# Attention in pairs of heads, convolution low parts on GpSimd, and an eighteenth FFN pair in a hybrid decoder layer

## The chip, the cores and the metric

One core of one Trainium2 chip. The metric is the device time of one execution in microseconds (us); the kernel before was run three times.

## The reference

One layer on 512 tokens of width 1024, all in float32:

```python
h = h + 0.5 * rmsnorm(swiglu(rmsnorm(h, g1), ffn1_w_in, ffn1_w_out), g1p)   # FFN1, hidden width 2816
mix = token_mixer(rmsnorm(h, gm), ...)                                      # below
h = h + rmsnorm(mix, gmp)
h = h + 0.5 * rmsnorm(swiglu(rmsnorm(h, g2), ffn2_w_in, ffn2_w_out), g2p)   # FFN2
gate = sigmoid(rmsnorm(h, gp) @ ple_w_gate)
h = h + rmsnorm(gate * (p @ ple_w_proj), gpp)

# token_mixer: one projection of u gives q_a k_a v_a z_a a_a b_a q_b k_b v_b q_i k_i w_i g_a g_b
qkv = silu(causal_conv(concat(q_a, k_a, v_a), conv_w))      # 4 taps, 1536 channels
o_a = gated_delta_rule(l2norm(q), l2norm(k), v, g, beta)    # 8 heads, chunks of 64, a triangular solve
score = sum_h w_i * relu(q_i . k_i)                         # indexer; the top 128 admissible keys per query
o_b = softmax(q_b . k_b over the selected keys) @ v_b       # 8 heads of 64, causal
mix = (sigmoid(g_a) * (o_a' @ w_br_a) + sigmoid(g_b) * (o_b @ w_br_b)) @ w_out
```

## The kernel before, in words

**Matmuls.** A float32 product is made as three: each operand is split into a high part and a low part (the remainder), and mm3 (L99 to L102) multiplies high by high, low by high and high by low. Weights come in chunks of 128x1024: wchunk (L84 to L93) loads raw, ScalarE casts it to the high part whi (L91), VectorE subtracts for the low part wlo (L92). There are two raw buffers and three of whi and wlo, so that the cast for one chunk waits until the chunk three before it has been multiplied. Transposes run on TensorE through tr (L108).

**FFN** (ffn, Seven). f counts 22 slices of 128 hidden columns, each with gate and up. An ordinary f is two tiles pgu of 24 matmuls of 512 columns (L418 and after). From f = 5 on, Seven.pair makes gate and up together with seven half-width products instead of eight, 84 matmuls of 256 columns (pfa, pfb, pfc, pfd). It needs the tiles t, sums of blocks of the input made once after f = 3. The output projection, out_proj, ends with put(0) and put(1), transposes of the next stage's first token tiles (ys), set between the last matmuls of the last token tile: put(0) behind the six matmuls with a = 0, put(1) behind the six with a = 2.

**The mixer.** The convolution's 12 chunks run one after the other (conv_mm: 24 matmuls into pc; conv_tr: transposes pct). Each pc takes a PSUM bank that is free again when VectorE has added the last tap (cy, L521) of the chunk two before. Beside them VectorE selects the top keys (MAX8 and MATCH_REPLACE). When the keys are normed (rk, on GpSimd), the decay and beta rows go through a transpose (prow), a copy (rowT) and a DMA to DRAM (rowd, L859), from which chunk_blocks loads them broadcast: DT (L813: a load, a select on GpSimd, a subtraction on VectorE, an exponential on ScalarE) and kbr (L809: two loads, a product on VectorE). The products pA (L824, L826) of four heads per block, two of which lie in rows 0 to 63 and two in rows 64 to 127 of the array, become BT and KQs. Diagonal blocks of BT go through DRAM (dgd) to solve(), 62 dependent VectorE steps (L924, L926), whose result goes through DRAM (zd) and back for the first pw matmuls of the delta rule.

**Attention** has 32 units: four pairs of heads, each with four token tiles (tt = 3, 0, 2, 1) and two heads. att_soft makes the score pat (L881, 128 to 512 columns), adds the bias on VectorE, and exponentiates on ScalarE into at; att_tr transposes at into ppt (one to four 128x128) and copies it to pt; att_pv multiplies with the values into pob (L911). Step i issues att_soft(i), att_tr(i - 2) and att_pv(i - 3). The tile tag at has three buffers that DT and rl share; pt has two. Behind attention come ptm (the last in-projection chunks) and pw.

A scheduler at build time orders every engine's queue; program order holds only where the code asks for it.

Of the kernel before, what the change touches and what calls it, by code (L numbers as in the profile page):

```python
# [32 lines left out]
def layer_kernel(ctx, tc, x, pT, wf1, wo1, wfm, wsm, wtm, wbr, wout, wf2, wo2, wgate, wproj,  # L33
# [17 lines left out]
    env = Env()  # L51

# [30 lines left out]
    def wchunk(src, n=1024, dst=None, eng=None):  # L83
        raw = wp.tile([128, 1024], F32, name="raw", tag="raw", bufs=2)  # L84
        SY.dma_start(raw[:, :n], src)
        if dst is None:
            hi = wp.tile([128, 1024], F32R, name="whi", tag="whi", bufs=3)
            lo = wp.tile([128, 1024], F32R, name="wlo", tag="wlo", bufs=3)
        else:
            hi, lo = dst  # L90
        A.copy(hi[:, :n], raw[:, :n])  # L91
        (eng or V).tensor_sub(lo[:, :n], raw[:, :n], hi[:, :n].bitcast(F32))  # L92
        return hi, lo  # L93
# [94 lines left out]
    def out_proj(nj, load, lhs, order1, order2, held, half, ys, gp, finish, free, evac=None, lead=0, held0=0, split=False):  # L188
# [28 lines left out]
        for ch, order in ((0, order1), (1, order2)):  # L217
# [14 lines left out]
            for tt in range(4):  # L232
                cut = ((0, 256), (256, 512)) if split and ch and tt == 3 else ((0, 512),)
                for i, (lo, hi) in enumerate(cut):
                    if i:
                        ps[tt] = axp("acc2")
                    for a, j in enumerate(order[n:]):
                        if ch and tt == 3:
                            with in_order() if env.puts else ExitStack():
                                m = part(ps[tt], tt, ws[a], j, n + a == 0, n + a == nj - 1, lo, hi)  # L240
                            if a in (0, 2):
                                put(a // 2, m)
# [142 lines left out]
    def ffn(fp, free, wf, wo, hsrc, u, gi, gn_i, first, hold=None):  # L385
# [31 lines left out]
        for f in range(nf, FT):  # L417
# [3 lines left out]
            if f >= 5:  # L421
                seven.pair(f, wf[2 * f], wf[2 * f + 1], hid)
                continue
# [288 lines left out]
    for tt in (3, 2, 1):  # L712
        S = 128 * (tt + 1)
        sc = tp.tile([128, S], F32, name=f"sc{tt}")
        for hd in range(8):
# [3 lines left out]
            rl = tp.tile([128, T], F32, name="rl", tag="at", bufs=3)  # L719
# [82 lines left out]
    def chunk_blocks():  # L802

        for c in range(4):
# [6 lines left out]
            for h4 in range(2):  # L811
                DT = tp.tile([128, 4, 128], F32, name="DT", tag="at", bufs=3)
# [28 lines left out]
    late = []  # L841
    for j in list(range(4, 8)) + list(range(4)) + list(range(8, 12)):
# [25 lines left out]
    drip(99)  # L868
    for j in (13, 14, 15):
        gate_tile(j)  # L870
        next(blocks)
# [4 lines left out]
    def att_soft(i):  # L876
# [6 lines left out]
        at = tp.tile([128, T], F32, name="at", bufs=3)  # L883
# [9 lines left out]
    def att_tr(i):  # L893
# [6 lines left out]
        pt = tp.tile([128, T], F32, name="pt", bufs=2)  # L900
# [37 lines left out]
    for i in range(len(units) + 3):  # L938
        if i < len(units):
            att_soft(i)  # L940
        if i in (2, 4, 6):
            next(blocks, None)
        if i == 7:
            for _ in blocks:
                pass
            ZC, XC, Z = solve()
        if i == 1:
            conv_tr(*late.pop())
        if 0 <= i - 2 < len(units):
            att_tr(i - 2)  # L950
        if 0 <= i - 3 < len(units):
            att_pv(i - 3)
# [175 lines left out]
    if True:  # L1128
# [33 lines left out]
        def load(ch, j, a):  # L1162
            w = wchunk(wout[ch, j], dst=xo.get(a) or (upper(tl) if ch or j > 1 else None))
            if (ch, j) == (1, 3):
# [5 lines left out]
                 sandwich_tail(h, ys, gnt, u2), lambda: (tail_pool.close(), mx_pool.close()), held0=2)  # L1170
# [129 lines left out]
```

## Time and profile before

| what | value |
|---|---|
| median of three runs | 1283.7 us (1282.6 to 1284.87) |
| the profiled execution | 1280.92 us, span 1279.1 us |
| TensorE (PE) | 1253.4 us busy, 98% |
| VectorE (DVE) | 883.5 us, 69% |
| ScalarE (ACT) | 567.0 us, 44% |
| GpSimd (POOL) | 66.2 us, 5% |
| granted TensorE clock, mean | 0.996 |

Times in rows are microseconds from the start of the span. A row of a timeline gives the start, the duration, the engine, the line, the operation, what it writes and reads, and in brackets how long the engine was idle before it and what ended that. Matmuls are pipelined and a record's end is modelled, so the time that a matmul takes is read from the start of one to the start of the next. A matmul of plain float32 (a score, a pA product) is two records.

### The profile page before, as it was taken

What the parts mean: (1) busy time and instruction counts of PE and PEld (TensorE: products, weight loads), DVE (VectorE), ACT (ScalarE), POOL (GpSimd) and SP (SyncE); (2) the same over time, 40 slices, a digit from 0 to 9 for tenths busy, and PEclk for the clock granted to TensorE, in tenths of its full rate; (3) what the DMA queues carried; (4) which work ended last, traced back from release to release, by engine and by line L of the source; (5) the groups of instructions that cost most, each with busy time, mean ns of one, the idle gap of its engine ahead of it and who ended that gap; (6) DMA issues with size and microseconds to landing.
All of it is one profiled execution on the core that took longest, in us unless ns stands there. A gap on an engine that the chain in (4) does not pass through costs nothing.

```text
span 1279.1 us, 19714 instructions
## 1 busy us (share of the span) xinstructions
PE 1253.4 (98%) x7885; PEld 1103.6 (86%) x7885; DVE 883.5 (69%) x1451; ACT 567.0 (44%) x914; POOL 66.2 (5%) x69
## 2 busy tenths in 40 slices
PE   6999999999999999989999999999999999999997
PEld 6999999988889888877678888779899999888886
DVE  6779999743372799976685544758699998623555
ACT  6334444752352443454554222344344445822353
POOL 0000000000010000031002001310000000000000
PEclk9999999999999999999999999999999999999999
DMA  6323333522442223244305544732433333433331
GB/s 214 126 66 112 109 111 100 181 82 94 147 156 84 66 68 116 91 116 124 92 1 133 164 158 157 230 116 83 134 108 106 99 106 123 144 93 113 115 116 66
DMA packets 59517, 147.76 MB, mean 116 GB/s; under 512 B 17761, under 2 KB 20257, under 8 KB 59425
## 3 DMA queue, kind: packets, MB, share of 16 engines
q1 hardware_dynamic: 58992, 144.93, 35.4%
q10 hardware_dynamic: 432, 1.57, 0.4%
q8 instruction: 62, 1.02, 0.3%
q14 instruction: 31, 0.25, 0.1%
HBM read 132.81 MB, written 13.66 MB: 115 GB/s over the span
## 4 chain that ended last, share of the span: by engine, by line
PE 89%; DMA 4%; DVE 4%; ACT 2%; issue 1%; POOL 0%; SPq 0%; DVEq 0%; POOLq 0%; ACTq 0%
PE acc L101 6%; PE acc L102 6%; PE acc L100 6%; PE p L101 3%; PE p L102 3%; PE p L100 3%; PE pfd L100 3%; PE pfb L100 3%; PE pfd L102 3%; PE pfd L101 3%; PE pfb L102 3%; PE pfb L101 3%; PE pfc L100 3%; PE pfc L101 3%; PE pfc L102 2%; PE ptm L100 2%
## 5 line engine op out<-in xcount | busy, mean ns | idle before, releaser
L92 DVE TENSOR_TENSOR wlo<-raw,whi 128x1024 fp32r<-128x1024 f32 x70 | 86.9, 1241 | 62.5 <-ACT whi L91 60.0
L91 ACT CAST whi<-raw 128x1024 fp32r<-128x1024 f32 x70 | 73.5, 1051 | 122.5 <-PE pc L101 35.3
L92 DVE TENSOR_TENSOR vlo<-raw,vhi 128x1024 fp32r<-128x1024 f32 x37 | 46.8, 1267 | 78.0 <-ACT vhi L91 78.0
L102 PE MATMUL acc<-vhi,hid 128*128 128x512 f32 x240 | 93.4, 389 | 0.0
L101 PE MATMUL acc<-vlo,hid 128*128 128x512 f32 x240 | 93.4, 389 | 0.0
L100 PE MATMUL acc<-vhi,hid 128*128 128x512 f32 x240 | 81.7, 389 | 0.0
L91 ACT CAST vhi<-raw 128x1024 fp32r<-128x1024 f32 x37 | 38.7, 1048 | 83.2 <-PE acc L102 72.5
L285 ACT CAST whi<-sb 128x1024 fp32r<-128x1024 f32 x26 | 27.3, 1049 | 83.9 <-PE pfc L101 75.1
L78 POOL TENSOR_TENSOR rinv<-ms,mhalf 128x1 f32<-128x1 f32 x32 | 19.4, 606 | 801.7 <-DVE ms L123 801.7
L100 PEld LDWEIGHTS acc<-vhi,hid 128*128 128x128 f32 x240 | 45.1, 188 | 9.4
L102 PEld LDWEIGHTS acc<-vhi,hid 128*128 128x128 f32 x240 | 45.1, 188 | 9.4
L101 PEld LDWEIGHTS acc<-vlo,hid 128*128 128x128 f32 x240 | 45.0, 188 | 9.4
L101 PE MATMUL ptm<-wlo,uhi 128*128 128x512 f32 x128 | 50.3, 393 | 0.0
L100 PE MATMUL ptm<-whi,uhi 128*128 128x512 f32 x128 | 50.0, 395 | 0.0
L102 PE MATMUL ptm<-whi,ulo 128*128 128x512 f32 x128 | 49.8, 391 | 0.0
L100 PE MATMUL pc<-uhi,whi 128*128 128x512 f32 x96 | 38.5, 401 | 3.9 <-ACT DT L818 3.9
L100 PE MATMUL pg<-uhi,whi 128*128 128x512 f32 x104 | 41.2, 396 | 0.0
L102 PE MATMUL pg<-uhi,wlo 128*128 128x512 f32 x104 | 40.9, 393 | 0.0
L101 PE MATMUL pg<-ulo,whi 128*128 128x512 f32 x104 | 40.7, 392 | 0.0
L286 DVE TENSOR_TENSOR hid<-gt,hid 128x512 fp32r<-128x512 f32 x44 | 29.5, 689 | 15.1 <-ACT hid L285 15.1
L102 PE MATMUL pc<-uhi,wlo 128*128 128x512 f32 x96 | 38.9, 405 | 0.0
L101 PE MATMUL pfd<-t,x 128*128 128x256 f32 x136 | 38.4, 282 | 0.0
(536 smaller groups left out, 4210.2 us busy)
## 6 DMA issues: line engine op xcount, KB each, us to landing
raw<-wf SPq DMA_DIRECT2D x52, 512.0 KB, 3.7
raw<-wo SPq DMA_DIRECT2D x44, 512.0 KB, 3.6
rawy<-wf SPq DMA_DIRECT2D x36, 512.0 KB, 3.8
raw<-wfm SPq DMA_DIRECT2D x28, 512.0 KB, 3.8
raw<-wtm SPq DMA_DIRECT2D x20, 512.0 KB, 3.7
gd<-gst SPq DMA_DIRECT2D x16, 256.0 KB, 2.1
raw<-wbr SPq DMA_DIRECT2D x8, 512.0 KB, 4.0
grl<-gd SPq DMA_DIRECT2D x16, 256.0 KB, 3.8
```

The lines of the kernel that those rows point to most:

```text
L78: G.tensor_tensor(out_, in_, e, op=ALU.pow)
L91: A.copy(hi[:, :n], raw[:, :n])
L92: (eng or V).tensor_sub(lo[:, :n], raw[:, :n], hi[:, :n].bitcast(F32))
L100: PE.matmul(ps, l[0], r[0], start=start, stop=False)
L101: PE.matmul(ps, l[0], r[1], start=False, stop=False)
L102: return PE.matmul(ps, l[1], r[0], start=False, stop=stop)
L285: A.copy(dst[0], src)
L286: V.tensor_sub(dst[1], src, dst[0].bitcast(F32))
```

## The change

Five edits:

- the subtraction for wlo of the 12 convolution chunks goes from VectorE to GpSimd (env.split);
- pairs start at f = 4 instead of f = 5 in both FFNs;
- put(1) of the two FFNs goes behind a = 3 instead of a = 2; the mixer's own call keeps a = 2;
- the tag at gets four buffers instead of three, pt four instead of two;
- attention issues two scores, then the transposes of the two units before, then the value products of the two before those.

```diff
     env = Env()
+    env.split = V
...
-        (eng or V).tensor_sub(lo[:, :n], raw[:, :n], hi[:, :n].bitcast(F32))
+        (eng or env.split).tensor_sub(lo[:, :n], raw[:, :n], hi[:, :n].bitcast(F32))
...
-                            if a in (0, 2):
-                                put(a // 2, m)
+                            if a in (0, at):
+                                put(min(a, 1), m)
...
-            if f >= 5:
+            if f >= 4:
                 seven.pair(f, wf[2 * f], wf[2 * f + 1], hid)
...
-                DT = tp.tile([128, 4, 128], F32, name="DT", tag="at", bufs=3)
+                DT = tp.tile([128, 4, 128], F32, name="DT", tag="at", bufs=4)
...
+    env.split = G
     for j in list(range(4, 8)) + list(range(4)) + list(range(8, 12)):
...
     drip(99)
+    env.split = V
...
-        pt = tp.tile([128, T], F32, name="pt", bufs=2)
+        pt = tp.tile([128, T], F32, name="pt", bufs=4)
...
-    for i in range(len(units) + 3):
-        if i < len(units):
-            att_soft(i)
-        if i in (2, 4, 6):
-            next(blocks, None)
-        if i == 7:
-            for _ in blocks:
-                pass
-            ZC, XC, Z = solve()
-        if i == 1:
-            conv_tr(*late.pop())
-        if 0 <= i - 2 < len(units):
-            att_tr(i - 2)
-        if 0 <= i - 3 < len(units):
-            att_pv(i - 3)
+    for p in range(len(units) // 2 + 2):
+        for i in (2 * p, 2 * p + 1):
+            if i < len(units):
+                att_soft(i)
+            if i in (2, 4, 6):
+                next(blocks, None)
+            if i == 7:
+                for _ in blocks:
+                    pass
+                ZC, XC, Z = solve()
+            if i == 1:
+                conv_tr(*late.pop())
+        for back, step in ((1, att_tr), (2, att_pv)):
+            for i in (2 * (p - back), 2 * (p - back) + 1):
+                if 0 <= i < len(units):
+                    step(i)
```

GpSimd's queue from the index scores to the DT selects, before (rk is the key norm, rq the query norm):

```order
L726 AFFINE_SELECT sc_4295<-sc_4295 128x128
L78 TENSOR_TENSOR rk<-ssk,mhalf 128x32
L814 AFFINE_SELECT DT<-DT 128x512 x3
L78 TENSOR_TENSOR rq<-ssq,mhalf 128x32
L814 AFFINE_SELECT DT<-DT 128x512
```

and now:

```order
L727 AFFINE_SELECT sc_4351<-sc_4351 128x128
L93 TENSOR_TENSOR wlo<-raw,whi 128x1024 x9
L79 TENSOR_TENSOR rk<-ssk,mhalf 128x32
L93 TENSOR_TENSOR wlo<-raw,whi 128x1024 x3
L815 AFFINE_SELECT DT<-DT 128x512 x4
L79 TENSOR_TENSOR rq<-ssq,mhalf 128x32
L815 AFFINE_SELECT DT<-DT 128x512
```

Nine low parts stand ahead of rk, three more ahead of the selects, and a fourth select ahead of rq.

VectorE's queue at the first DT, about 566 to 575 us, before (the three cy are the taps of the tenth convolution chunk):

```order
L521 SCALAR_TENSOR_TENSOR cy<-pc,prm,cy 128x511
L816 TENSOR_TENSOR DT<-DT,gcs 128x512
L810 TENSOR_TENSOR kbr<-kT,kbr 128x512
L863 TENSOR_SCALAR ssq<-ssq 128x32
L521 SCALAR_TENSOR_TENSOR cy<-pc,prm,cy 128x510
L548 TENSOR_TENSOR vbt<-pct,rkb 128x4x128
L816 TENSOR_TENSOR DT<-DT,gcs 128x512 x2
L521 SCALAR_TENSOR_TENSOR cy<-pc,prm,cy 128x509
L810 TENSOR_TENSOR kbr<-kT,kbr 128x512
```

and now:

```order
L817 TENSOR_TENSOR DT<-DT,gcs 128x512
L547 TENSOR_REDUCE ssq<-sq 128x4x2
L817 TENSOR_TENSOR DT<-DT,gcs 128x512 x2
L865 TENSOR_SCALAR ssq<-ssq 128x32
L817 TENSOR_TENSOR DT<-DT,gcs 128x512
L93 TENSOR_TENSOR wlo<-raw,whi 128x1024
L811 TENSOR_TENSOR kbr<-kT,kbr 128x512
L522 SCALAR_TENSOR_TENSOR cy<-pc,prm,cy 128x511
L811 TENSOR_TENSOR kbr<-kT,kbr 128x512
L549 TENSOR_TENSOR vbt<-pct,rkb 128x4x128
L522 SCALAR_TENSOR_TENSOR cy<-pc,prm,cy 128x510
L522 SCALAR_TENSOR_TENSOR cy<-pc,prm,cy 128x509
```

Four DT subtractions now stand ahead of the first kbr product, and all three taps behind it.

TensorE's queue in attention, some 625 us into the span, before (numbers behind a name tell its buffers apart):

```order
L881 MATMUL pat_6164<-hz_4110 128x512
L108 MATMUL ppt_6173<-cst_78,at_6048 128x128 x2
L881 MATMUL pat_6182<-hz_4110 128x128
L911 MATMUL pob_6141<-vb_4771,pt_6139 128x64 x3
L911 MATMUL pob_6178<-vb_4771,pt_6158 128x64 x2
L108 MATMUL ppt_6191<-cst_78,at_6148 128x128 x4
L881 MATMUL pat_6201<-hz_4110 128x128
L108 MATMUL ppt_6210<-cst_78,at_6166 128x128 x4
```

and now:

```order
L884 MATMUL pat_6234<-hz_4166 128x128
L884 MATMUL pat_6243<-hz_4166 128x128
L914 MATMUL pob_6225<-vb_4827,pt_6190 128x64 x3
L109 MATMUL ppt_6252<-cst_78,at_6199 128x128 x4
L914 MATMUL pob_6266<-vb_4827,pt_6218 128x64 x2
L109 MATMUL ppt_6259<-cst_78,at_6208 128x128 x4
L884 MATMUL pat_6273<-hz_4166 128x384
L884 MATMUL pat_6282<-hz_4166 128x384
```

The two scores of a pair of heads stand side by side.

## Rows read from the trace of the kernel before

**Rows 1.** The page: busy time, share and instructions of each engine.

```profile
PE 1253.4 (98%) x7885; PEld 1103.6 (86%) x7885; DVE 883.5 (69%) x1451; ACT 567.0 (44%) x914; POOL 66.2 (5%) x69
```

**Rows 2.** Timeline of TensorE in FFN1: f = 4, first two pairs, put(1).

```profile
64.14 0.39 PE L100 MATMUL pgu<-uhi,whi 128*128 128x512 f32 x1
...
75.02 0.28 PE L100 MATMUL pfa<-uhi,whi 128*128 128x256 f32 x1
...
85.01 0.28 PE L100 MATMUL pfa<-uhi,whi 128*128 128x256 f32 x1
...
363.12 1.09 PE L108 MATMUL put<-cst,ys 128*128 128x128 f32 x8 [0.85 <-DVE ys L156]
```

**Rows 3.** Timeline of VectorE in FFN1: the last of the tiles t.

```profile
47.84 1.21 DVE L286 TENSOR_TENSOR t<-trys,t 128x1024 fp32r<-128x1024 f32 x1
```

**Rows 4.** Timeline of TensorE at the twelfth convolution chunk.

```profile
570.14 0.50 PE L824 MATMUL pA<-kbr,kT 64*128 64x128 f32 x4 [0.45 <-DVE kbr L810]
...
575.31 0.77 PE L100 MATMUL pc<-uhi,whi 128*128 128x512 f32 x1 [3.91 <-ACT DT L818]
...
579.71 0.39 PE L101 MATMUL pc<-ulo,whi 128*128 128x512 f32 x1
```

**Rows 5.** Timeline of VectorE: convolutions, and one row from 692.

```profile
546.27 1.23 DVE L92 TENSOR_TENSOR wlo<-raw,whi 128x1024 fp32r<-128x1024 f32 x1
...
569.40 0.68 DVE L810 TENSOR_TENSOR kbr<-kT,kbr 128x512 f32<-128x512 f32 x1
...
574.43 0.73 DVE L521 SCALAR_TENSOR_TENSOR cy<-pc,prm,cy 128x509 f32<-128x509 f32 x1
...
692.17 2.20 DVE L92 TENSOR_TENSOR wlo<-raw,whi 128x1024 fp32r<-128x1024 f32 x1 [1.25 <-ACT whi L91]
```

**Rows 6.** Timeline of GpSimd: rk, the third DT select, two-input operations.

```profile
544.97 5.43 POOL L78 TENSOR_TENSOR rk<-ssk,mhalf 128x32 f32<-128x32 f32 x1 [77.99 <-DVE ssk L848]
...
572.70 1.04 POOL L814 TENSOR_SCALAR_AFFINE_SELECT DT<-DT 128x512 f32<-128x512 f32 x1 [0.18 <-DMA DT<-rowd]
...
809.94 2.15 POOL L1151 TENSOR_TENSOR grl<-grl,ybm 128x512 f32<-128x512 f32 x1 [3.91 <-DVE grl L1150]
818.25 2.55 POOL L1151 TENSOR_TENSOR grl<-grl,ybm 128x512 f32<-128x512 f32 x2 [6.16 <-DVE grl L1150]
```

**Rows 7.** Stretches: busy us of PE, PEld, DVE, ACT, POOL; clock, DMA.

```profile
572.00:580.00 8.00, 4.69 (x12) 3.73 (x13) 6.71 (x13) 3.17 (x4) 6.96 (x3) 0.57 0.40 109
637.00:667.00 30.00, 29.95 (x180) 20.73 (x180) 24.32 (x94) 20.02 (x68) 0.00 (x0) 1.00 0.00 1
```

**Rows 8.** DMA: issue of rowd on SyncE; of tile DT, issue to landing.

```profile
561.54 0.53 SPq L859 DMA_DIRECT2D rowd<-rowT  x1
...
DMA to landing us min/median/max: 3.0/3.5/5.6
```

**Rows 9.** Groups by line on TensorE, 607 to 667: busy us, mean ns.

```profile
L881 PE MATMUL pat<-hz 64*128 64x128 f32 (+3 forms) x62 | 24.5, 475 | 0.0
```

**Rows 10.** Timeline of TensorE: pA of two heads at once, of one.

```profile
591.82 0.49 PE L824 MATMUL pA<-kbr,kT 64*128 64x128 f32 x4
592.04 0.49 PE L826 MATMUL pA<-qT,kT 64*128 64x128 f32 x4
...
609.18 0.38 PE L824 MATMUL pA<-kbr,kT 64*128 64x128 f32 x2
609.41 0.38 PE L826 MATMUL pA<-qT,kT 64*128 64x128 f32 x2
```

**Rows 11.** Timeline of VectorE: first and last step of the solve, its transposition.

```profile
635.61 0.19 DVE L924 TENSOR_TENSOR ztmp<-dz 128x31 f32<-128x31 f32 x1 [0.81 <-DMA dz<-dgd]
...
674.53 0.22 DVE L926 TENSOR_TENSOR dz<-dz,ztmp 128x31 f32<-128x31 f32 x1
...
683.39 1.25 DVE L935 STREAM_TRANSPOSE dz<-dz 128x1024 f32<-128x1024 f32 x1 [1.12 <-DMA dz<-zd]
```

**Rows 12.** Timeline of TensorE: the first matmuls of pw.

```profile
690.50 1.68 PE L996 MATMUL pw<-dz,BT 32*32 32x32 f32 x94
```

More of the change, by code (lines that the diff above doesn't have):

```diff
@@ L186, in put, with out_proj @@
                 env.puts.pop(tt)()
-    def out_proj(nj, load, lhs, order1, order2, held, half, ys, gp, finish, free, evac=None, lead=0, held0=0, split=False):
+    def out_proj(nj, load, lhs, order1, order2, held, half, ys, gp, finish, free, evac=None, lead=0, held0=0, split=False, at=3):
         sums = [sp.tile([128, 3], F32, name=f"sums{tt}", bufs=1) for tt in range(4)]
@@ L718, in layer_kernel @@
                 PE.matmul(pd[:, :S], qiT[hd][:, tt * 128:(tt + 1) * 128], kiT[i][:, :S], start=i == 0, stop=i == 1)
-            rl = tp.tile([128, T], F32, name="rl", tag="at", bufs=3)
+            rl = tp.tile([128, T], F32, name="rl", tag="at", bufs=4)
             A.activation(rl[:, :S], pd[:, :S], AF.Relu)
@@ L882, in att_soft @@
                   start=True, stop=True)
-        at = tp.tile([128, T], F32, name="at", bufs=3)
+        at = tp.tile([128, T], F32, name="at", bufs=4)
         nm = sp.tile([128, 1], F32, name="nm", bufs=4)
@@ L1169, in layer_kernel @@
                  lambda k, tk: (mgh[:, k, tk], mgl[:, k, tk]), list(range(4)), list(range(4)), 4, False, ys, gpt,
-                 sandwich_tail(h, ys, gnt, u2), lambda: (tail_pool.close(), mx_pool.close()), held0=2)
+                 sandwich_tail(h, ys, gnt, u2), lambda: (tail_pool.close(), mx_pool.close()), held0=2, at=2)
         u = u2
```

## The prediction

> **What bounds the kernel now.** I read the page first: TensorE is busy for 1253.4 of 1279.1 us [rows 1], so time is won by giving it less to do, by closing one of its few gaps, or by letting two of its matmuls run at once. Then I read the timeline of TensorE for gaps at the places that the diff touches. One stands where FFN1 ends: the transposes of ys wait 0.85 us [rows 2]. The large one is at 571: the four pA products wait 0.45 us, and the first matmul of the twelfth convolution chunk 3.91 us [rows 4]. The row gives an exponential of DT as its releaser, but that line's work had long ended; what ended at 575.2 is the last convolution tap on VectorE (cy, 509 columns, 574.43 + 0.73) [rows 5], which frees the PSUM bank that this chunk (two after the tap's own) writes. VectorE does its work in order, and ahead of that tap stand three DT subtractions, each behind a GpSimd select, each behind a DMA: the third select begins at 572.70, released by a DMA [rows 6]. After the gap the clock is low: 0.57 is the mean grant of the stretch 572 to 580 [rows 7], and ten matmuls take from 575.31 to 579.71 [rows 4], 0.44 us apiece against the 0.227 that 48 ordinary ones show (64.14 to 75.02, [rows 2]): 2.1 us more. The gap thus costs 0.45 + 3.91 + 2.1 = 6.4 us.
>
> **Attention** (607 to 667) shows no gap, so there I asked what TensorE does and who is next. VectorE is busy for 24.3 of the 30 us from 637 on [rows 7], and carries the triangular solve from 635.61 to 674.53 [rows 11] between the softmax steps. On the solve wait a few DMAs, and on those the first pw matmul at 690.50 [rows 12]; between attention and pw lie 128-column weight chunks (ptm) that need neither.
>
> **The change, part by part.** The sum is made against the profiled execution, 1280.9 us (span 1279.1 and 1.8 around it). The median shown, 1283.7, stands 2.8 above; I add that at the end.
>
> 1. One more FFN pair. An ordinary f is 48 matmuls, 64.14 to 75.02 = 10.88 us; a pair is 84 of half the width, 75.02 to 85.01 = 9.99 us [rows 2]. Twice (two FFNs) 0.89 = **1.8 us less**. The pair needs its t tiles: the last is made at 47.84 + 1.21 [rows 3], 15 us before 64.14, so the earlier start is covered. Its added work on VectorE and ScalarE is what the 17 pairs behind it do at the same pace. Without that cover the pair would wait for t; nothing shows it.
>
> 2. put(1) six matmuls later. Six times 0.227 is 1.36 us. That is more than the idle 0.85 in FFN1 [rows 2], which ends with VectorE's ys; TensorE then works on meanwhile and arrives after ys: **0.9 us less** (0.85 and a little of the restart). FFN2 has no such wait in the trace, the mixer's call keeps its place: nothing. What it delays is the next part of the transposes by less than they were early.
>
> 3. Low parts on GpSimd. Twelve subtractions of 1.23 us leave VectorE [rows 5], 15 us off a queue that has no gap worth the name until 556. On GpSimd I have no such row. Two 128x512 ones took 2.55 us [rows 6], so a 1024-wide one is 2.6 us; the slow end is the one of 2.15 us, 4.3 us doubled. I take 2.6, with 4.3 in the range. A chunk's period is 24 matmuls and a few transposes, 5.9 us, so both ends keep up; three buffers let the cast before it be made when the chunk three before ends, some 10 us ahead of use, so neither end lets TensorE wait for the low part itself. What counts is the queue: the order puts rk (5.43 us, [rows 6]) behind nine low parts and the DT selects behind all twelve. The twelfth is cast when the ninth chunk ends, two chunks ahead of 570 [rows 4], about 558; with 2.6 it ends at 560.7, before any DT lands.
>
> What moves then is the chain rows, rowd, DT, kbr. In the order prow stands a whole chunk earlier, so rowd (before at 561.54, [rows 8]) goes at some 556 to 559; four DT loads follow directly, then, behind one weight load that waits for the twelfth low part, the four kbr loads, at 561 to 564. A DT load took 3.0 to 5.6 us from issue [rows 8], and kbr, half as large, I estimate alike: kbr is there at 565 to 569 where the multiply before was at 569.40 [rows 5]. On VectorE four DT subtractions now stand before the multiply, and behind it the three taps, the second kbr and vbt: by the rows 0.68 + 0.68 + 0.68 + 3 x 0.74 = 4.3 us until the last tap. With kbr at 565.5 the bank is free at 569.8 and nothing of the 6.4 us is left; with 569 it is free at 573.3, the gap is 2.5 us, and I count no long low clock after a gap that much smaller. With GpSimd at 4.3 us the raw buffers come free some 3 us later, kbr at 571, and the gap is as before or 1 us longer. I take **3.8 us less** (6.4 less to 1 more), near the late end of kbr, because four loads now share the way that three shared.
>
> What the row shows on the two engines together: at 692.17 a low part on VectorE took 2.20 us instead of 1.23 while GpSimd worked on zs [rows 5]. The Trainium skill (SBUF — State Buffer, the section on the two separate sides) has this as an exclusive lock: a VectorE operation with two SBUF inputs and a GpSimd one never run at once, the second waits for the whole of the first. The row agrees in direction, with 1.0 us. By that rule the twelve low parts could hold VectorE up to 12 x 2.6 = 31 us, against the 15 us that leave it, and part 3 would bring nothing.
>
> 4. Two units at a time. The heads of a unit pair lie in rows 0 to 63 and 64 to 127 of the array. Before, a score (pat) never follows a score in this stage; in the order of after, nearly all stand in pairs. Whether two halves run at once is shown by the pA products: each head issues its two records of one line and then two of the next, so a group of four is two heads. From the group of four at 591.82 to the next at 592.04 are 0.22 us; from a group of two at 609.18, one head alone, to the next at 609.41 are 0.23 [rows 10]. Twice the work goes by in the same time. The scores are 24.5 us in the stage [rows 9]; half can hide, **12.2 us, is the ceiling**. It is not reached, as VectorE and its DMAs come next. In the first half of the stage the last chunk blocks need DT loads, which now stand behind the stores dgd, and the solve cannot start before them: I see it at 634.6 to 636.6 against 635.61, no gain. In the 30 us behind that VectorE waits 5.7 us [rows 7], mostly for scores, which the pairs can remove in part: the solve ends 3 to 6 us earlier than 674.53. Its result, transposed at 683.39 + 1.25 [rows 11], is there 5.9 us before pw (the second copy that pw reads lands somewhat later, which no row here shows), so TensorE sets the start of pw as long as the stage shrinks by less than that slack and the solve's gain together. I take **5 us less**, the middle of 0 to 10.
>
> The two extra at and two extra pt buffers cost nothing: a score's successor waits for them less. The longer queues that wait behind them are in the order: two scores ahead of the transposes, which VectorE must reduce first, 0.69 us each at 512 columns; other pairs' transposes and value products stand between.
>
> Sum: 1.8 + 0.9 + 3.8 + 5.0 = 11.5 less: 1280.9 - 11.5 = 1269.4 in a profiled execution, **1272 us** as a median.
>
> **The rivals.**
> - *TensorE alone sets attention.* For it: no gap in the stage, pA's halves side by side. Against: VectorE at 81% from 637 on. Then 12.2 instead of 5: 1265.
> - *The solve alone sets it.* If its start comes late by what it gains later, pw is where it was, and TensorE waits at pw: 0 instead of 5: 1277. For it: DT behind dgd.
> - *GpSimd holds VectorE up*, or takes 4.3 us: part 3 brings nothing, the rest stays: 1276. For it: the row at 692.17. Against: the taps read PSUM, and VectorE has 15 us more room. If the two last come together: 1281, no change.
> - *Holes in attention; slower.* VectorE is in order. If three DT subtractions stand in its queue before the scores' softmax while their DMAs are late, TensorE, which now has two scores done and nothing to transpose, stands three times as it did at 571, 3.9 + 2.1 us with the low clock: 18 us. Then 1280.9 - 1.8 - 0.9 - 3.8 - 5 + 18 = 1287, as a median 1290. It decides when a DT lands later than the work of two units that is queued ahead, some 4 us. For it: the loads behind the stores. Against: the added at buffer lets DT load earlier.
> - *The scores do not run side by side* since each takes a whole bank and 512 columns, where pA has 128: about 1.5 us from fewer changes of shape instead of 5, so 1275 to 1276; inside the range.
>
> **How the numbers follow.** Forecast, with the last rival beside it: 0.47 (1268 to 1276). TensorE alone 0.14 (1265); solve alone 0.17 (1277); GpSimd 0.10 (1276), of which with the solve 0.04 at 1281; holes 0.12 (1290). The range 1263 to 1281 leaves out the holes and a tail below, 0.15 to 0.2. A difference under 0.2% (2.6 us) is about what a measurement of this kernel cannot tell from none. Faster than 1281.1 are all but the holes and the two that come together: 0.82; same 0.06; slower 0.12.
>
> **What would show it.** Part 1: pfa starts 9.9 to 10 us after the f=4 start at 64.1, and no gap. Part 2: no idle ahead of put in FFN1. Part 3: POOL rows of wlo at 2.6 us; the first matmul of the twelfth chunk with under 2.7 us idle, and a grant near 1.0 behind it. Part 4: score records of two heads with starts a few ns apart; gaps of TensorE in 607 to 660; the solve's last step at 665 to 670; pw at some 11 us earlier than 690.5. The forecast falls if VectorE's two-input operations are long in the convolutions, if TensorE shows idle of some us at DT, or if the scores' records follow each other at 0.5 us.

## The result, and the profile after

The change made the kernel faster, by about half of what was forecast (6.1 us of 11.5): 1277.6 us median of 13 executions (1268.2 to 1282.1) against 1283.7 for the kernel before in the same comparison (13 executions, 1280.1 to 1284.9). The ratio is 0.9943, 95% interval 0.992 to 0.9967. The forecast of 1272 lies 5.6 us below, the range of 1263 to 1281 holds it.

The spread is part of the result. The kernel before stays within 0.4%; the changed one covers 1.1%, and its time follows TensorE's mean granted clock over the span: 1268.16 at 0.996, 1272.3 at 0.991, 1277.6 at 0.987, 1282.07 at 0.983. Two profiled executions of it, 1277.7 (span 1275.9) and 1267.1 (span 1265.3, below called the second profile), show where this arises. Executions more than 1.5% above the fastest of their kernel are left out of the medians and ratios here: three at 1313 to 1318 us with a clock of 0.964 to 0.971 (one of old_loop below, two of the kernel before), none of them profiled, and two at 2501.8 (old_loop) and 7055.5 us (old_loop_late_dt).

The page of the changed kernel answers [rows 1]; busy time, share and instructions:

```profile
PE 1250.6 (98%) x7957; PEld 1109.7 (87%) x7957; DVE 886.8 (70%) x1459; ACT 570.6 (45%) x920; POOL 95.9 (8%) x81
...
PEclk9999999999999999999599999999999999999999
```

The second line is the granted clock in 40 slices of 31.9 us. One slice, 606 to 638, stands at 5 where its neighbours have 9: that is the attention stage.

How far ahead of the kernel before each mark stands, by its start in the traces (negative: earlier), and what each stretch added:

| stretch, up to | forecast for it | changed, 1277.7 | second profile, 1267.1 |
|---|---|---|---|
| FFN1, first acc matmul | -0.9 | -2.0 | -1.8 |
| put(1), to the first matmul of p behind it | -0.9 | -1.0 | -1.1 |
| start of the twelfth convolution chunk | -3.8 with the next line | -2.2 | -2.8 |
| end of the convolutions | (as above) | 0.0 | -1.6 |
| gates, to the last pg | 0 | -1.5 | -1.5 |
| attention, to the first ptm behind it | -5 | **+3.1** | **-7.5** |
| pw and the mixer, to pgu of FFN2 | 0 | -0.2 | +1.7 |
| FFN2's pairs, to its first acc | -0.9 | -1.1 | -1.1 |
| FFN2's end | 0 | +1.7 | +1.9 |
| sum | -11.5 | -3.2 | -13.8 |

(Of FFN1's 2.0 and 1.8, 0.9 and 0.6 lie ahead of f = 4, where the diff changes nothing.) So the terms ahead of attention came out near their size, the attention stage gained half as much again as forecast or else lost, in the same program, and FFN2's end gave back what nobody had charged.

Timeline of TensorE, changed kernel: start, duration, line, tiles, and in brackets the idle time ahead with its releaser.

```profile
63.27 0.28 PE L101 MATMUL pfa<-uhi,whi 128*128 128x256 f32 x1
...
83.00 0.28 PE L101 MATMUL pfa<-uhi,whi 128*128 128x256 f32 x1
...
361.48 1.06 PE L109 MATMUL put<-cst,ys 128*128 128x128 f32 x8
...
570.09 0.47 PE L101 MATMUL pc<-uhi,whi 128*128 128x512 f32 x1 [2.13 <-DVE cy L522]
...
571.01 0.63 PE L101 MATMUL pc<-uhi,whi 128*128 128x512 f32 x1
...
600.03 1.13 PE L884 MATMUL pat<-hz 64*128 64x512 f32 x4
601.09 0.66 PE L109 MATMUL pct<-cst,vfm 128*128 128x128 f32 x4
...
608.42 1.64 PE L884 MATMUL pat<-hz 64*128 64x384 f32 x2 [1.72 <-DVE nm L888]
...
687.67 2.21 PE L1000 MATMUL pw<-dz,BT 32*32 32x32 f32 x128
...
1215.26 0.50 PE L101 MATMUL pj<-whi 128*128 128x512 f32 x1 [1.53 <-DVE ys L208]
```

The first two rows stand two pairs apart, 19.73 us or 9.87 for one, where [rows 2] had 9.99. put(1) has lost its idle of 0.85. The twelfth chunk now waits 2.13 us where [rows 4] had 0.45 and 3.91, and its clock still falls for a while: matmuls of 0.63 us begin at 571.01. Two scores (four records) now go by in 601.09 - 600.03 = 1.06 us. One alone took 0.95 in the kernel before, from its start to that of the next matmul:

```profile
592.27 1.02 PE L881 MATMUL pat<-hz 64*128 64x512 f32 x2
593.22 0.50 PE L100 MATMUL pg<-uhi,whi 128*128 128x512 f32 x1
```

So they do run side by side. Then come two idles that the trace of the kernel before does not have: 1.72 us in attention, ended by VectorE's nm (a reduction of the softmax), and 1.53 us at 1215, at FFN2's end.

What stands behind the first is on VectorE's and GpSimd's timelines:

```profile
605.13 0.17 DVE L892 RECIPROCAL rs<-sm 128x1 f32<-128x1 f32 x1 [0.23 <-ACT at L890]
607.47 0.69 DVE L817 TENSOR_TENSOR DT<-DT,gcs 128x512 f32<-128x512 f32 x1 [2.17 <-POOL DT L815]
608.07 0.28 DVE L888 CUSTOM_DVE_ANT_0 at<-pat,cst 128x128 f32<-128x128 f32 x1
```

```profile
606.79 0.64 POOL L815 TENSOR_SCALAR_AFFINE_SELECT DT<-DT 128x512 f32<-128x512 f32 x1 [19.68 <-DMA DT<-rowd]
```

The load of this DT was issued at 602.57 and released GpSimd's select at 606.79, 4.2 us later. VectorE, which works in order, stood 2.17 us at the subtraction on DT; the softmax step of a finished score (at, 608.07) stood behind it, and TensorE, whose next score waits for that step, behind that. The score itself needs nothing of this DT; DT is merely ahead in VectorE's queue.

The wait of VectorE is not new. In the kernel before it stood as long at the same DT, the sixth of eight:

```profile
615.98 0.69 DVE L816 TENSOR_TENSOR DT<-DT,gcs 128x512 f32<-128x512 f32 x1 [2.15 <-POOL DT L814]
```

There TensorE had value products, pA products and a score to do meanwhile, and no idle came of it. What the change took away is that work in front; VectorE waited as long for DT before.

What follows the idle is in a table of stretches of the changed kernel: busy us of PE, PEld, DVE, ACT, POOL (with counts), granted clock, DMA share and GB/s.

```profile
604.00:608.00 4.00, 2.70 (x21) 1.74 (x17) 1.51 (x7) 1.10 (x5) 0.64 (x1) 1.00 0.56 161
608.00:642.00 34.00, 33.58 (x133) 25.58 (x133) 16.43 (x67) 16.21 (x51) 1.27 (x2) 0.50 0.18 47
642.00:646.00 4.00, 4.00 (x33) 3.52 (x34) 3.88 (x19) 4.00 (x15) 0.00 (x0) 0.96 0.00 0
```

The grant is 1.00 until the idle, 0.50 (1.2 of 2.4 GHz) for the 34 us behind it, though TensorE is busy for 33.58 of them, and 0.96 again from 642. The second profile has the same idle at the same place, and the low clock is over after some 8 us:

```profile
606.47 0.91 PE L884 MATMUL pat<-hz 64*128 64x384 f32 x2 [1.76 <-DVE nm L888]
```

```profile
608.00:614.00 6.00, 6.00 (x34) 5.28 (x34) 2.84 (x14) 2.62 (x9) 0.45 (x1) 0.61 0.38 88
614.00:616.00 2.00, 2.00 (x7) 0.91 (x6) 1.42 (x5) 1.62 (x5) 0.48 (x2) 0.50 0.24 65
616.00:620.00 4.00, 4.00 (x31) 3.40 (x29) 4.00 (x14) 2.00 (x8) 0.34 (x1) 0.98 0.26 68
624.00:654.00 30.00, 29.07 (x220) 23.16 (x218) 26.53 (x109) 22.35 (x81) 0.00 (x0) 1.00 0.06 19
```

No other difference of that size between the two executions shows in this stage: +3.1 against -7.5 us. The last row also shows who is next at full clock: VectorE, 26.53 of 30 us, where [rows 7] had 24.32.

### The profile page after: what moved, and what is told of

Read it like the earlier page. It is cut to its first block, busy times and chain, and to the rows that moved or that the text cites. A ratio compares the mean times of both kernels' runs of the same rounds, so it can differ in the third digit from the quotient of the medians.

```text
span 1275.9 us, 19873 instructions
## 1 busy us (share of the span) xinstructions
PE 1250.6 (98%) x7957; PEld 1109.7 (87%) x7957; DVE 886.8 (70%) x1459; ACT 570.6 (45%) x920; POOL 95.9 (8%) x81
## 4 chain that ended last, share of the span: by engine, by line
PE 90%; DVE 4%; DMA 4%; ACT 1%; issue 1%; SPq 0%; POOL 0%; DVEq 0%; POOLq 0%; ACTq 0%
PE acc L102 7%; PE acc L103 7%; PE acc L101 7%; PE p L102 3%; PE p L103 3%; PE pfd L101 3%; PE pfd L103 3%; PE pfb L101 3%; PE pfd L102 3%; PE p L101 3%; PE pfc L102 3%; PE pfb L103 3%; PE pfb L102 3%; PE pfc L101 3%; PE pfc L103 3%; PE ptm L102 2%
## 5 line engine op out<-in xcount | busy, mean ns | idle before, releaser
L93 DVE TENSOR_TENSOR wlo<-raw,whi 128x1024 fp32r<-128x1024 f32 x58 | 72.0, 1242 | 62.9 <-ACT whi L92 52.3
L102 PE MATMUL pfd<-t,x 128*128 128x256 f32 x144 | 40.6, 282 | 0.0
L101 PE MATMUL pfd<-t,x 128*128 128x256 f32 x144 | 40.6, 282 | 0.0
```

Source lines behind the costliest of these rows:

```text
L93: (eng or env.split).tensor_sub(lo[:, :n], raw[:, :n], hi[:, :n].bitcast(F32))
L101: PE.matmul(ps, l[0], r[0], start=start, stop=False)
L102: PE.matmul(ps, l[0], r[1], start=False, stop=False)
```

## The experiments

The theory after the first profile: the pairs save TensorE time as meant, but behind one idle at a late DT the clock falls, and it comes back late where only thin work follows (64-row scores, 128-column transposes). Rivals: the pairs themselves keep the clock low; the saving never was one; the low parts on GpSimd explain the gains and losses around it. Edits are against the changed kernel unless said otherwise.

**The old attention loop** in the changed kernel, with all else kept (four at and pt buffers too).

```diff
-    for p in range(len(units) // 2 + 2):
-        for i in (2 * p, 2 * p + 1):
...
+    for i in range(len(units) + 3):
...
+        if 0 <= i - 2 < len(units):
+            att_tr(i - 2)
+        if 0 <= i - 3 < len(units):
+            att_pv(i - 3)
```

> The changed kernel with attention's loop as it was before (one score, then the transposes of two units back, then the value product of three back); all other edits stay, the four buffers too. Theory A (the gap at 606.7, where VectorE stands behind a late DT, drops TensorE's clock to half for 34 us, and that takes back what the pairs win): without pairs no such gap, clock 0.99 or more in 607 to 642; the time is what the other edits leave: 5.2 us won up to the twelfth chunk, 2.1 in FFN2, 1.7 lost in the tail, so 1283.7 - 5.6 = 1278, all executions within 3 us. Theory B (the pairs win nothing because VectorE and the solve set the stage): 1274 to 1276, faster than the changed kernel's middle. Theory C (the low clock comes to this chip by chance, whatever the order): a spread of over 10 us between executions here too.

Measured: ratio 0.9937 (0.9922 to 0.9953), executions of 1274.5 to 1278.1 us, clock 0.996 to 0.998. In its profile no TensorE idle from 600 to 667 is longer than 0.45 us, and the clock holds:

```profile
608.00:660.00 52.00, 52.00 (x304) 36.04 (x302) 37.38 (x148) 33.61 (x109) 1.91 (x3) 1.00 0.12 35
```

So the idle comes with the new loop. VectorE's wait does not: here too it stands at the sixth DT, and TensorE works through it.

```profile
609.92 0.69 DVE L817 TENSOR_TENSOR DT<-DT,gcs 128x512 f32<-128x512 f32 x1 [1.97 <-POOL DT L815]
```

The trace is as theory A had it, the median of 1275.6 lies in theory B's range. As medians the two loops are level (0.9937 and 0.9943): by the traces, what the pairs save and what the clock takes about cancel.

**The pair loop alone**: the kernel before with the new loop and the four buffers, none of the other parts.

```diff
-            rl = tp.tile([128, T], F32, name="rl", tag="at", bufs=3)
+            rl = tp.tile([128, T], F32, name="rl", tag="at", bufs=4)
...
-    for i in range(len(units) + 3):
+    for p in range(len(units) // 2 + 2):
...
```

> The kernel before with the attention loop in pairs and the four buffers alone (low parts on VectorE, 17 pairs, put as before). By the changed kernel's two profiles the pairs win 10 us from the start of attention to pw where the clock comes back soon, and lose 2 where it stays low: 1273 to 1275 in the executions with a mean clock of 0.994 or more, 1284 to 1286 in those at 0.985. If the pairs only pay together with the other edits: 1281 or more throughout.

Measured: ratio 0.9984 (0.9966 to 1.0002) over 12 executions, 1273.4 to 1285.6 us, clock 0.984 to 0.993. Alone, the part that was to bring 5 us is not distinguishable from nothing as a median. Its executions again follow the clock, much as expected: 1273.4 at 0.992, 1285.6 at 0.984. In the profiled one (1275.1 at 0.993) the stage from the last pg to ptm gained 7.5 us, as in the second profile, though it has an idle of 1.41 us too. In the same profile the convolution gap is 3.27 us, hardly shorter than the 3.91 of [rows 4]: so the buffers alone do not account for the shorter one of the changed kernel.

**Filling the gap**: the pA products of the block whose DT is late (c = 2, h4 = 1) are done three times, so TensorE has work while VectorE waits; the last time counts, the others are useless.

```diff
-                for i2 in range(2):
+                for i2 in [0, 1] * (3 if (c, h4) == (2, 1) else 1):
```

> The changed kernel with the pA products of the block whose DT is late (third chunk, second half) done three times over into the same bank: about 1.8 us more work for TensorE where it stood idle for 1.7 us, the result is the same. Theory A: no idle of over 1 us at 606, granted clock 1.0 through 607 to 642, all executions near 1268 to 1271, though there is more work. Theory B: 1278 to 1280, the work is added. Theory C: the spread of the changed kernel, 1268 to 1282, plus up to 1.8.

Measured: ratio 0.9896 (0.9875 to 0.9917), median 1270.0. It did not do what it was made for: the idle is still 1.49 us, later, at 611.05. But the low clock ended early in the profile, and pw started 10.3 us ahead of the kernel before:

```profile
612.00:617.00 5.00, 5.00 (x23) 4.31 (x24) 1.60 (x9) 1.88 (x6) 0.64 (x1) 0.51 0.27 67
617.00:622.00 5.00, 5.00 (x28) 3.99 (x28) 3.66 (x16) 2.86 (x8) 0.64 (x1) 0.81 0.22 63
```

More useless work and less time; but an idle that moved and shrank at once doesn't say which of the two did it. Some 1 us of the gain is not attention's: the idle ahead of pj in FFN2 is 0.43 us here instead of 1.53.

**One block earlier**: the block c = 2, h4 = 1 issued ahead of attention.

```diff
+    next(blocks)
     obt = mx.tile([128, 4, T], F32, name="obt", tag="oa")
...
-            if i in (2, 4, 6):
+            if i in (2, 4):
```

> The changed kernel with that block issued ahead of attention's first unit (so its DT load stands ahead of two weight loads), and the two others one step earlier each. Theory A: VectorE never stands behind DT at 605 to 607, no gap there, clock 1.0, all executions at 1266 to 1270. Theory B: 1276 to 1279. Theory C: the spread 1268 to 1282 stays.

Measured: ratio 0.9949 (0.993 to 0.9969), 1272.5 to 1281.0 us. A miss: the next block takes the place. TensorE idles 3.35 us ahead of a score at 615.50 (VectorE's pt copy stands behind the next DT), and the clock is 0.50 from 615.5 to 642. Moving one late block moves the hole.

**All blocks earlier**: two blocks behind each of the last three gates, the eighth ahead of attention, none inside.

```diff
         gate_tile(j)
         next(blocks)
+        next(blocks)
+    next(blocks, None)
...
-            if i in (2, 4, 6):
-                next(blocks, None)
```

> The changed kernel with two chunk blocks behind each of the last three gate tiles instead of one, so that all eight stand ahead of attention's units (the scheduler still mixes their last products with the first scores). Theory A (VectorE stands behind a late DT, TensorE goes idle, its clock drops): no DT subtraction between scores, no idle of over 1 us from 600 on, clock 1.0, the solve starts some 15 us earlier; the attention stage ends when TensorE ends it: 12 us under the changed kernel's slow executions, all at 1264 to 1269. Theory B (the pairs themselves bring the low clock): idle gone, the clock still half for some 30 us, 1277 to 1280.

Measured: ratio 0.9906 (0.9878 to 0.9933), median 1270.6. The idle at DT is gone from attention; two of 1.34 and 1.87 us now stand among the gates' dense chunks (pg, waiting for VectorE's KQs), the clock is 0.66 from 604 to 609 and 1.00 from 609 to 660. One of six executions was still at 1280.2 (0.987).

**The same with put(1) back in FFN2**, for the idle at 1215. FFN1 keeps the later place.

```diff
-                 ys, gp, sandwich_tail(h, ys, gn, u2), free)
+                 ys, gp, sandwich_tail(h, ys, gn, u2), free, at=3 if hold is None else 2)
```

> As blocks_first, and FFN2's second transposes (put) go back behind a = 2; FFN1's stay behind a = 3. If the 1.5 us that a PLE product (pj) waits for ys at 1215 in the changed kernel comes from that move: no such idle, 1.5 us under blocks_first, and put waits for nothing. If it comes from elsewhere: the same time as blocks_first within 0.5 us.

Measured: ratio 0.9879 (0.9857 to 0.9901), median 1267.4, five of six executions at 1265.7 to 1267.9. It has the lowest median of the study and beats the kernel before and the changed kernel's 13 executions; against the two of the changed kernel beside it (1267.1 and 1272.4) nothing is decided. The idle ahead of pj is gone, and from FFN2's first acc matmul to the end nothing is lost. Its profiled execution happens to be the sixth (1275.2, clock 0.989): one idle of 1.04 us in attention, at 623, and then

```profile
622.00:640.00 18.00, 16.92 (x69) 12.61 (x69) 10.55 (x48) 8.81 (x30) 0.00 (x0) 0.54 0.00 1
642.00:660.00 18.00, 17.73 (x138) 14.07 (x138) 17.41 (x73) 14.57 (x54) 0.00 (x0) 1.00 0.01 1
```

Half as many matmuls in the first 18 us as in the second. The hole is not a late DT this time, but it is the same kind of wait: VectorE stands at the first step of the triangular solve, which waits for the load of dz, and the softmax step of a score stands behind it.

```profile
622.21 0.19 DVE L929 TENSOR_TENSOR ztmp<-dz 128x31 f32<-128x31 f32 x1 [1.30 <-DMA dz<-dgd]
```

**One block fewer ahead**, the last two called together behind unit 2, with the put of the version above.

```diff
-        next(blocks)
-    next(blocks, None)
+        if j < 15:
+            next(blocks)
...
-            if i == 7:
+            if i == 2:
                 for _ in blocks:
                     pass
+            if i == 7:
```

> As blocks_first_put2, with one chunk block fewer ahead of the last gate tile: it comes with attention's units 2 and 3. The waits of the gate tiles for KQs (2.5 and 3.2 us there) should go, and a DT subtraction stands between the first scores again. Theory A: if TensorE is not idle for 1 us there, 1264 to 1266 in all executions, the fastest yet; if it is, some executions at 1272 to 1278 again.

Measured: ratio 0.9897 (0.9883 to 0.9912), median 1269.6 of four. A miss: 1264 to 1266 was expected. TensorE idles 2.4 us ahead of a value product (pob), with VectorE behind the last DT, and 1.9 and 0.4 us among the gates; the clock is 0.57 from 612 to 623. Not better than all blocks ahead.

**Low parts back on VectorE**, all else as changed.

```diff
-    env.split = G
+    env.split = V
```

> The changed kernel with the 12 convolution low parts back on VectorE. If these edits of the queue won the 2.2 us at the twelfth chunk: its first matmul is idle for 3 to 4 us again with a low clock behind it, start of attention 2 to 4 us later than in the changed kernel. If GpSimd's low parts rather slowed VectorE (the lock): VectorE's rows there are shorter and the chunk starts earlier. Attention's clock may fall or not as in the changed kernel by theory A, so the time alone, 1270 to 1285, tells little.

Measured: ratio 0.9946 (0.9922 to 0.997), 1268.4 to 1281.0 us: no difference to the changed kernel. The convolution gap is as short without the low parts on GpSimd:

```profile
569.98 0.47 PE L101 MATMUL pc<-uhi,whi 128*128 128x512 f32 x1 [1.90 <-ACT DT L819]
```

That is not what was expected of it (3 to 4 us again if the edits of the queue had won), so the shorter gap isn't the low parts' doing. VectorE's timeline and GpSimd's in the changed kernel show in addition that the two engines hold each other up:

```profile
538.39 2.21 DVE L850 TENSOR_SCALAR ssk<-ssk 128x32 f32<-128x32 f32 x1
```

```profile
538.16 2.40 POOL L93 TENSOR_TENSOR wlo<-raw,whi 128x1024 fp32r<-128x1024 f32 x1 [3.81 <-ACT whi L92]
```

ssk, which takes 0.17 us with the low parts on VectorE, ends here with the GpSimd operation at 540.6. The taps are not held up: 743 ns apiece against 738 (the 509-column ones, 460 to 560).

**A made delay, old loop**: two useless VectorE additions (2048 and 1024 columns) in unit 4's softmax, to make an idle where the old loop has none.

```diff
+        if i == 4:
+            hold = mx.tile([128, 2048], F32, name="hold", tag="ol")
+            for n in (2048, 1024):
+                V.tensor_tensor(hold[:, :n], nm.to_broadcast([128, n]), nm.to_broadcast([128, n]), op=ALU.add)
```

> The kernel with the old attention loop (run old_loop, 1276.9) and two useless VectorE operations of 2.1 and 1.1 us behind the score of unit 4, about where the changed kernel's VectorE stands behind DT; the result is the same. Theory A: TensorE is idle for 1 to 2 us near 610, and the clock falls to half behind it as with the pairs: 1280 to 1290, spread over 8 us. Theory B: an idle time alone costs its own 1 to 3 us, no low clock in the stage: 1278 to 1280, spread as in old_loop.

Measured: ratio 0.994 (0.9925 to 0.9955), clock 0.996 to 0.999. No idle arose on TensorE, so this says nothing about the clock; it says that the old loop had work queued that covers such a delay, as it covers the wait at DT.

**The changed kernel again**, beside these on their chip.

> The changed kernel once more, for another profile of it. Theory A: the idle of 1.7 us at 606 is there in every execution, what differs is how long the clock stays low behind it: near 1268 with under 8 us of it, near 1280 with over 30. Theory C: executions near 1268 have no idle there at all.

Measured: 1267.11 (clock 0.996, the second profile) and 1272.44 (0.992). In the one that was profiled an idle (1.76 us) recurs at the same place, the length of the low clock doesn't.

**A late DT in the old loop**: a useless 1 MB copy in DRAM on SyncE's queue ahead of that one DT load. Against the old loop's kernel.

```diff
+                if (c, h4) == (2, 1):
+                    SY.dma_start(spare, gd[12:16])
                 SY.dma_start(DT, rowd[0, c, 4 * h4:4 * h4 + 4][None].to_broadcast([128, 4, 128]))
```

> The kernel of old_loop (old attention loop, all else as changed) with a useless 1 MB copy from DRAM to DRAM put on SyncE's queue just ahead of the DT load of the third chunk's second half, so that this DT lands some 4 to 6 us later; the result is the same. Theory A in its first form (an idle time of TensorE in this stage drops the clock for up to 34 us, pairs or not): an idle of 2 us or more at 606 to 612, clock at half behind it, executions spread over 8 us or more, 1281 to 1290. Theory D (the idle drops the clock for about 6 us, as behind the gap at 575 before; it is the pairs that keep it low for longer): idle of the same size, clock low for 5 to 8 us, all executions within 4 us, 1279 to 1283. If the old loop covers the delay: no idle, 1276 to 1278.

Measured: ratio 1.0283 (1.0267 to 1.0299), median 1319.8 of four, clock 0.963 to 0.965. DT is released 8.1 us after its issue, VectorE waits 4.57 us for it, and TensorE has one idle of 1.98 us:

```profile
613.36 0.90 PE L109 MATMUL ppt<-cst,at 128*128 128x128 f32 x3 [1.98 <-DVE pt L907]
```

```profile
600.00:611.00 11.00, 10.55 (x67) 7.13 (x64) 6.26 (x22) 5.23 (x14) 0.00 (x0) 1.00 0.72 229
612.00:702.00 90.00, 88.64 (x283) 59.69 (x284) 39.58 (x150) 34.38 (x108) 1.65 (x3) 0.50 0.06 15
704.00:730.00 26.00, 26.00 (x242) 21.70 (x242) 11.47 (x22) 10.93 (x17) 3.73 (x3) 1.00 0.58 108
```

The clock is half for 90 us, in which TensorE is busy for 88.64, until the dense weight chunks of ptm (they start at 702.8). The time is 44 us longer (1319.8 against 1275.6, the old loop's median), twenty times the idle; by an estimate from the row, 88.64 us of busy time at half the clock are 44 us more than the same work takes at the full one. So theory D, in which the pairs keep the clock low, fails: without them it stays low longest.

**The same with dense work behind it**: 24 useless 128x512 matmuls ahead of unit 8's score. Against the kernel with the late DT.

```diff
+        if i == 8:
+            for r in range(24):
+                PE.matmul(pa, u[0][:, r % 8, 0:128], u[0][:, r % 8, 0:512], start=True, stop=True)
```

> The kernel of old_loop_late_dt (old attention loop, one DT made late; 1320.0, clock at half from 611 to 704) with 24 useless 128x512 matmuls of all 128 rows ahead of unit 8's score, in that score's own bank; the result is the same. They stand some 10 us behind the idle and are 5.5 us of work at full clock, 10.3 at half. Theory E (TensorE in this stage, one score or short transposes and value products at a time, does not bring the clock back by itself, and dense work does, as ptm did at 704): the clock is back within these 24 or just behind them, 1.0 from 630 on at the latest, and the time falls by 20 us or more though work is added: 1288 to 1298. Theory F (the clock stays low for a time of its own, some 90 us, whatever TensorE does): 1.0 again only beyond 700, and 1325 to 1331.

Measured: ratio 1.0059 (1.004 to 1.0078), median 1290.9, clock 0.991 to 0.994: 29 us less than without the added work, in every one of six executions. The 1 MB copy is still there, so by itself it accounts for no more of the 44 us than the 15 that remain. The idle is the same (2.03 us), and the dense matmuls begin at 621.65:

```profile
614.56 0.55 PE L109 MATMUL ppt<-cst,at 128*128 128x128 f32 x3 [2.03 <-DVE pt L910]
...
621.65 5.53 PE L889 MATMUL pat<-uhi 128*128 128x512 f32 x15
```

```profile
620.00:625.00 5.00, 5.00 (x16) 4.10 (x16) 2.94 (x8) 1.70 (x5) 0.64 (x1) 0.50 0.14 29
625.00:630.00 5.00, 5.00 (x26) 3.91 (x25) 0.09 (x1) 0.31 (x1) 0.00 (x0) 0.94 0.01 3
630.00:690.00 60.00, 60.00 (x333) 43.27 (x333) 40.40 (x148) 33.65 (x103) 0.00 (x0) 1.00 0.24 42
```

The clock rises while they run (0.94 from 625 to 630) and holds for the thin work that follows, as theory E had it. What half a clock does to that work is in the groups by line (busy us, mean ns over four widths): scores without the dense work from 612 to 702, and with it from 630 to 690.

```profile
L887 PE MATMUL pat<-hz 64*128 64x256 f32 (+3 forms) x50 | 35.4, 811 | 0.0
```

```profile
L890 PE MATMUL pat<-hz 64*128 64x512 f32 (+3 forms) x48 | 19.3, 482 | 0.0
```

811 ns apiece against 482; [rows 9] had 475.

## Why the prediction was right, and where not

**FFN pairs: right**, mis-sized a little. 0.89 was forecast for each; FFN2 gained 1.14 in both profiles, FFN1 1.1 from f = 4 on.

**put(1): right in FFN1, wrong in FFN2.** FFN1's idle of 0.85 is gone, and 1.0 to 1.1 us are gained where 0.9 was forecast. "FFN2 has no such wait in the trace ... nothing" failed. FFN2's call goes through the same default and also got the later place. The transposes themselves do not come later there, and neither do VectorE's takeover (ulo) and, behind it in its queue, ys, which reads acc and so frees a bank: all keep their distance of 4.9 to 5.0 us from the kernel before, which is FFN2's lead at its first acc matmul. What moved is TensorE's order around them: eighteen acc matmuls now stand between put(0) and put(1) instead of twelve, and fewer of the last projection (pj). So the last acc matmul starts 6.35 us earlier than before, and TensorE is sooner at the pj matmul that needs the bank. First the kernel before, then the changed one:

```profile
1213.30 1.04 PE L108 MATMUL put<-cst,ys 128*128 128x128 f32 x8
...
1216.69 0.39 PE L102 MATMUL acc<-xo,hid 128*128 128x512 f32 x1
...
1219.39 0.68 DVE L207 TENSOR_TENSOR ys<-acc,gp 128x512 f32<-128x512 f32 x1
```

```profile
1208.32 1.03 PE L109 MATMUL put<-cst,ys 128*128 128x128 f32 x8
...
1210.34 0.39 PE L103 MATMUL acc<-xo,hid 128*128 128x512 f32 x1
...
1214.52 0.68 DVE L208 TENSOR_TENSOR ys<-acc,gp 128x512 f32<-128x512 f32 x1
```

That pj matmul, which had no idle before, waits for ys: 1.53 us in one profile, 1.64 in the other. FFN2's end gave back 1.7 and 1.9 us. With the put of FFN2 restored the idle is gone and so is the loss; the median falls from 1270.6 to 1267.4, more than the 1.7 us that the trace gives, in ranges that overlap. The step asked where the removed wait was, and not what the moved transposes let run ahead.

**Low parts on GpSimd: the right size, but not by this edit.** Their duration was 2.40 us (2.6 forecast), kbr's multiply came at 565.95 (forecast 565 to 569), and the gap and its low clock shrank by 2.2 to 4.4 us (3.8 forecast). But low_on_vector has the same gap of 1.9 us and the same time, with the order of the kernel before: its third DT subtraction and its last tap still come one behind the other, only 5.3 us earlier than before, where the pA products are 3.3 us earlier. The term belongs to something else in the change; the four buffers with the pair loop alone still had 3.27 us, and which of the rest shortens the gap was not isolated. That VectorE waits for GpSimd is real but rare: from 460 to 560 ssk's 2.0 us is the largest case, 1.05 us on a 256-column step of the key selection the next. The Trainium skill (SBUF — State Buffer, the section on the two separate sides) has an exclusive lock between GpSimd and those VectorE operations that use the port pair the two share, the later one blocked until the earlier one has ended; ssk's row agrees to the tenth of a microsecond, while the taps, at 743 ns against 738, are not held. The rival built on the hold-up (1276) thus has the outcome for this part, nothing gained, but not by its cause: TensorE is busy for all of 460 to 560 with the low parts on either engine, so VectorE's time there is no bound.

**Attention pairs: the mechanism right, the size somewhat low, and the clock left out.** The scores run side by side; at nearly full clock the stage gained 7.5 us (forecast 5, from 0 to 10), and VectorE is next, as said. The Trainium skill (TensorEngine Tiling (Array Packing), Theoretical Speedup) puts two row tiles of up to 64 rows at up to twice the speed; 1.06 us for two scores against 0.95 for one agrees. The rival in which the solve alone sets the end is refuted. In the second profile the solve's last step came 14.5 us earlier, 8.7 of it because the whole stage began earlier and 5.8 within the stage (forecast 3 to 6). Its result, transposed at 668.57 + 1.25, was there 5.2 us before pw began at 675.05, right behind the last ptm matmul: TensorE set the start of pw.

```profile
659.98 0.21 DVE L929 TENSOR_TENSOR dz<-dz,ztmp 128x31 f32<-128x31 f32 x1
```

That is the last step, against 674.53 in [rows 11].

**The holes: the rival was right in kind and mis-sized in both factors.** The prediction had its condition (a DT landing later than the work queued ahead, some 4 us; this one took 4.2 from issue to select), its place and its chain, and gave it 0.12 at 1290 with three holes of 3.9 + 2.1 us. What came was one hole of 1.7 us, so the forecast's sign held. The sum holds no term for it, since attention showed no gap of TensorE; VectorE's wait of 2.15 us at DT stood in the trace of the kernel before all the same, covered by work that the new loop moved. And the failing term of the rival is the 2.1 us of low clock: it was carried over from [rows 4, 7], where 512-column matmuls follow the gap and the clock is back after ten of them. In attention no such work follows, and the low clock lasted 8 us, 34 us, or, in the old loop with the late DT, 90 us. Between the two profiles that is 10.6 us. The first profile has the median's time: its attention stands 8.1 us behind the forecast, FFN2's end 1.7. That the median still fell inside the range is in part luck, since the sum had no term for either.

**What stays open.** Why the same idle in the same program is followed by 8 us of low clock in one execution and 34 in the other: none of the runs tells. Nor is the cause of the shorter gap at 570 settled. And blocks_first_put2 still falls into the low clock in the one execution that was profiled, behind an idle of 1.0 us at the solve's first load; in its five others, with a clock of 0.995 to 0.998, whether that idle is there is not known. A version that loads the solve's blocks earlier too was not made.

## What to carry to other kernels

Price an idle of TensorE by what follows it: in these runs it cost itself and some 2 us ahead of dense matmuls, and up to 44 us ahead of a stage of thin ones, so look at the granted clock stretch by stretch, in more than one execution. An engine that shows no gap may be covering another one's wait: before you reorder its queue, look for the waits that the old order hides. Before making an engine's queue deeper or its producer faster, find the operations in the in-order queue between them that wait for a DMA, and issue them ahead of the stage or leave enough work in front. And where an edit sits in a shared helper with a new default, follow each of its callers, and look at what it lets run ahead as well as at what it delays.

## What the runs showed of the hardware

- A fall to half clock that outlasts its cause: after an idle of 1.98 us the grant was 0.50 for 90 us in which TensorE was busy for 98% of the time by the profile. A busy share near one is no sign of a full clock.
- Added work that pays: with 24 matmuls of 128x512 put in from 621.65 on, the grant was 0.50 from 620 to 625, 0.94 from 625 to 630 and 1.00 after, and the kernel was 29 us faster.
- An idle doesn't always do it: at the twelfth chunk 1.63 us (second profile) left the grant at 1.00, with 2.13 us (first profile) it was 0.79 over the stretch 567 to 575; in attention 1.04 us were followed by 0.54 over 18 us.
- The GpSimd subtraction of 128x1024 takes 2.40 us, against 1.22 on VectorE.
